# One Trainium2 core: the convolution's accumulator in two tiles, every second low half of the K and V weights by DMA, and the S5 bodies and the last V columns moved

## The chip, the cores and the metric

The kernel runs on one core of one Trainium2 chip. The metric is the time on the device in microseconds (us) of one execution; the kernel before was timed three times and the median is 2125.04 us (2120.92 to 2128.39). The engines of a core are TensorE (PE in the profile, PEld is its weight load), VectorE (DVE), ScalarE (ACT), GpSimd (POOL) and SyncE (SP), which here only starts transfers.

## The reference

One layer of a hybrid trunk in float32 over 256 tokens of width 2048: a gated convolution group and an S5 (state space) group side by side, attention to 256 memory tokens, and a layer of experts (PEER).

```python
hn = rms_norm(h, norm_mix_g)
proj = hn @ w_in                                  # 2048 -> 1024 conv_a, 1024 conv_gate, 1024 ssm_u
c = causal_depthwise_conv(conv_a * sigmoid(conv_gate), conv_w, conv_b)      # width 31, 1024 channels
c = layer_norm(c, conv_ln_g, conv_ln_b);  yc = c * sigmoid(c)
y = s5_scan(ssm_u) + d * ssm_u                    # complex states, 64 groups of 64
z = gelu(y);  ys = z * sigmoid(z @ ssm_glu_w)
h = h + concat([rms_norm(yc, g_conv), rms_norm(ys, g_ssm)]) @ w_out
mem_n = rms_norm(mem, mem_norm_g);  k, v = split(mem_n @ w_kv_mem)          # 2048 -> 2048 + 2048
h = h + softmax(q k / sqrt(512)) v @ w_o          # q from rms_norm(h) @ w_q_mem, 4 heads
h = h + peer(rms_norm(h))                         # 16 experts of 16384 for each of 8 heads and token
out = rms_norm(h, final_norm_g)
```

## The kernel before

Every large product goes through `linear()` (line 146). It takes a weight in columns of 512, and each column in tiles of two times 128 rows, 512 KB a tile. A tile is loaded by SyncE's queue into `w_raw` (five buffers, line 153). ScalarE rounds it to `w_hi` (line 162, three buffers), VectorE takes the difference `w_lo = w_raw - w_hi` (line 163, three buffers), and TensorE makes three products of each piece, high by high, low by high and high by low, into a PSUM tile `mm`: lines 172 to 174 where tokens are the rows of the result, lines 181 to 183 where channels are. Of the eight tiles of a column in w_in, K and V the last one is multiplied whole in float32 (lines 140 and 143), without a split.

Each engine runs its own instructions in a fixed order. That order is made when the program is built, by a scheduler that goes by priorities; the loads and splits of weights are lifted ahead of the matmuls by `AHEAD = 500`, the S5 work by `S5_AHEAD = 700`, and the convolution, which stands late in the code, fills what VectorE has free.

The front part of the kernel, up to the experts, runs through these stages: w_in (the S5 columns, then the convolution's columns and gate), the K columns from 191 us, the V columns, Gelu and the gate product of S5 (`ev_glu`, weight `ssm_glu_w`), the norm of the S5 group (`group_norm`, line 527), the first half of w_out's rows, which needs the S5 group alone (`korder` 4 to 7, result into `h1_dram`), the second half of w_out from 551 us, which needs the convolution's group, and then attention. The S5 group has eight bodies (`s5_body`, called by `s5_next()`), each of 128 channels: four were called among the w_in columns and one behind each of the four K columns. A body uses working tiles that go by tags, `s5a` to `s5d`, and its sine tables come from ScalarE.

The convolution (lines 560 to 576) is 31 steps for each of eight groups of 128 channels, 248 instructions on VectorE into one tile `acc` of eight groups. Then come a mean over the channels (`chan_sum`, matmuls with ones), the variance (`squares`, `chan_rstd`), Silu on ScalarE, and the group norm, whose rounded halves `aT_hi`, `aT_lo` are the upper part of the input of w_out (`yT`).

Of the kernel before, what the change touches and what calls it, by code (L numbers as in the profile page):

```python
# [9 lines left out]
F32 = mybir.dt.float32  # L10
# [10 lines left out]
P = 128  # L21
# [45 lines left out]
LAG = 2  # L67
R_BY = ('AAAA', 'AAVA')
# [3 lines left out]
def trunk(ctx, tc, a, out, dbg=None):  # L72
# [48 lines left out]
    with ExitStack() as wctx:  # L121
        atx = wctx.enter_context(ExitStack())
        wp = wctx.enter_context(tc.tile_pool(name="wp", bufs=3, side="right"))
# [22 lines left out]
        def linear(x, w, c0, ncol, evac, rows_out, kt=KT, korder=None, ahead=AHEAD, whole=None, cols=None):  # L146
            xh, xl = x
            js = korder or range(kt // KG)
            for n, (c, w_) in enumerate(cols or [(c, 512) for c in range(c0, c0 + ncol, 512)]):
                ncb = w_ // P  # L150
                ps = [psm.tile([P, 512] if rows_out else [P, 2, T], F32, name="mm", tag="mm") for _ in range(2)]
                for m, j in enumerate(js):
                    with tc.high_priority(offset=ahead):
                        raw = wp.tile([P, KG, w_], F32, name="w_raw", bufs=5)
                        SY.dma_start(raw, w[j * KG * P:(j + 1) * KG * P, c:c + w_].rearrange("(k p) c -> p k c", p=P))
# [40 lines left out]
        with ExitStack() as mctx:  # L196
# [316 lines left out]
            def squares(src):  # L513
                out = []
                for j in range(2):
                    t = s5w.tile([P, 4, T], F32, name="sqh", tag="s5b")
                    S.activation(t, src[:, 4 * j:4 * j + 4, :], AF.Square)
# [9 lines left out]
            def group_norm(src, col, hi, lo):  # L527
                r = chan_rstd(chan_sum(squares(src)))
                for j in range(2):
                    for q in range(4 * j, 4 * j + 4):  # L530
                        V.scalar_tensor_tensor(src[:, q, :], src[:, q, :], colv[:, col, q:q + 1], r, op0=ALU.mult,
                                               op1=ALU.mult)
                    split(hi[j], lo[j], src[:, 4 * j:4 * j + 4, :])
# [15 lines left out]
            group_norm(uT, 4, yT[0][2:], yT[1][2:])  # L549
# [10 lines left out]
            acc = mp.tile([P, CQ, T], F32, name="acc")  # L560
            for k in range(CW):
                for q in range(CQ):
                    src = cpad[:, q, k:k + T]
                    if k == 0:
                        V.tensor_scalar(acc[:, q, :], src, cwT[:, q, 0:1], colv[:, 0, q:q + 1], op0=ALU.mult,
                                        op1=ALU.add)
                    else:
                        V.scalar_tensor_tensor(acc[:, q, :], src, cwT[:, q, k:k + 1], acc[:, q, :],  # L568
                                               op0=ALU.mult, op1=ALU.add)
            mean = chan_sum([acc[:, :4, :], acc[:, 4:, :]])  # L570
            V.tensor_sub(acc, acc, bc(mean[:, None, :], [P, CQ, T]))
            r = chan_rstd(chan_sum(squares(acc)))
            V.tensor_mul(acc, acc, bc(r[:, None, :], [P, CQ, T]))
            for q in range(CQ):
                S.activation(acc[:, q, :], acc[:, q, :], AF.Silu, bias=colv[:, 2, q:q + 1],
                             scale=colv[:, 1, q:q + 1])
            group_norm(acc, 3, yT[0][:2], yT[1][:2])
# [575 lines left out]
```

## Time and profile before

| what | value |
|---|---|
| median of three runs | 2125.04 us (2120.92 to 2128.39) |
| the profiled execution | 2121.98 us |
| its span in the trace | 2120.0 us |
| granted clock of TensorE, mean | 0.972 |
| busy: TensorE, VectorE, ScalarE, GpSimd | 1970.8 (93%), 1760.7 (83%), 1024.5 (48%), 736.2 us (35%) |

The trace is of one execution; its times are from the span's start. The granted clock is the share of TensorE's full speed. Matmuls are pipelined, so the distance of two starts, not the length of one, is what a matmul takes. Shares over the whole span mix stages with different limits, so the stretches are read one by one.

### The profile page before, as it was taken

To read this page: it belongs to the slowest core of one execution; us is meant where nothing else is said; L and a number is where in the kernel's file an instruction comes from. 1 tells how busy PE (TensorE), PEld (TensorE's weight loads), DVE (VectorE), ACT (ScalarE), POOL (GpSimd) and SP (SyncE) were. 2 spreads that over 40 slices of the span, in tenths; PEclk is the share of its full clock that TensorE was granted. 3 is DMA by queue.
4 is the path that set the end of the run, shared out by engine and by line. 5 is a ranking of instruction groups with operands and counts; after the bars stand their busy time and mean duration, and the time that the engine had idled before them with its cause. 6 is when DMAs were issued, how large, how long until landed. Compare 5 with 4: busy or idle time off the path is not lost.

```text
span 2120.0 us, 32032 instructions
## 1 busy us (share of the span) xinstructions
PE 1970.8 (93%) x11619; PEld 1698.4 (80%) x11619; DVE 1760.7 (83%) x2855; ACT 1024.5 (48%) x1746; POOL 736.2 (35%) x548
## 2 busy tenths in 40 slices
PE   8998798999999999899999999689879999999997
PEld 7987786668799988788888888577667888888886
DVE  5789999987665566999986667998888999899997
ACT  5764544436454454333333333578793444444444
POOL 0000000000000002535446665543218877677772
PEclk9999989999999999999999999899999999999998
DMA  7554454554865476798999999998629999999995
GB/s 246 166 179 154 125 149 130 161 177 139 291 222 193 140 232 221 283 321 319 317 336 402 402 406 391 370 327 275 205 90 318 373 348 337 348 336 340 336 340 187
DMA packets 199390, 563.41 MB, mean 266 GB/s; under 512 B 32050, under 2 KB 40866, under 8 KB 199105
## 3 DMA queue, kind: packets, MB, share of 16 engines
q1 hardware_dynamic: 141888, 318.08, 45.5%
q0 software_dynamic: 57344, 243.30, 30.5%
q8 instruction: 91, 1.49, 0.3%
q14 instruction: 67, 0.54, 0.1%
HBM read 549.38 MB, written 11.93 MB: 265 GB/s over the span
## 4 chain that ended last, share of the span: by engine, by line
PE 48%; DVE 25%; issue 13%; POOL 6%; DMA 5%; ACT 2%; SPq 0%; DVEq 0%; POOLq 0%; ACTq 0%
PE acc L1100 8%; PE acc L1101 8%; PE acc L1099 8%; DVE u L861 6%; POOL u L859 5%; PE mm L183 4%; PE mm L181 4%; PE mm L182 4%; DVE acc L568 3%; DVE w_lo L163 3%; PE mm L174 2%; PE mm L173 2%; PE mm L172 2%; PE y L932 1%; DMA hnT<-ib_dram 1%
## 5 line engine op out<-in xcount | busy, mean ns | idle before, releaser
L861 DVE SCALAR_TENSOR_TENSOR u<-u,hnF 128x1280 f32<-128x1280 f32 x256 | 388.6, 1520 | 86.0 <-DMA u<-in_peer_u,uidx 84.6
L1064 POOL DMA_INDIRECT v<-in_peer_v,vidx x256 | 385.7, 1507 | 178.5 <-DVE accg L1066 68.5
L859 POOL DMA_INDIRECT u<-in_peer_u,uidx x256 | 308.1, 1204 | 328.2 <-DVE u L861 254.0
L162 ACT CAST w_hi<-w_raw 128x1024 fp32r<-128x1024 f32 (+2 forms) x228 | 231.4, 1018 | 289.1 <-PE mm L182 125.7
L901 PE MATMUL sy<-hnT,ut 128*128 128x256 f32 x1536 | 357.0, 385 | 7.9 <-ACT ut L897 7.3
L163 DVE TENSOR_TENSOR w_lo<-w_raw,w_hi 128x1024 fp32r<-128x1024 f32 (+2 forms) x228 | 270.8, 1190 | 111.5 <-ACT w_hi L162 111.3
L901 PEld LDWEIGHTS sy<-hnT,ut 128*128 128x128 f32 x1536 | 287.3, 193 | 48.6 <-ACT ut L897 11.9
L103 ACT CAST vh<-vr 128x1472 fp32r<-128x1472 f32 x128 | 183.2, 1431 | 271.0 <-PE acc L1100 165.8
L1100 PE MATMUL acc<-vh,wl 128*128 128x512 f32 (+1 forms) x768 | 296.7, 386 | 4.4 <-DVE wl L1090 4.3
L183 PE MATMUL mm<-aT_hi,w_lo 128*128 128x256 f32 x960 | 273.2, 293 | 27.2 <-DVE w_lo L163 27.1
L1101 PE MATMUL acc<-vl,wh 128*128 128x512 f32 (+1 forms) x768 | 295.9, 386 | 0.0
L742 POOL TENSOR_TENSOR hnT<-aT_hi,aT_lo 128x1024 f32<-128x1024 f32 (+1 forms) x2 | 3.8, 1908 | 814.5 <-ACT w_hi L162 814.5
L181 PE MATMUL mm<-aT_hi,w_hi 128*128 128x256 f32 x960 | 279.0, 294 | 4.0 <-DVE sg L264 2.3
L1099 PE MATMUL acc<-vh,wh 128*128 128x512 f32 (+1 forms) x768 | 276.5, 385 | 3.2 <-ACT vh L103 2.2
L182 PE MATMUL mm<-aT_lo,w_hi 128*128 128x256 f32 x960 | 276.4, 290 | 0.0
L104 DVE TENSOR_TENSOR vl<-vr,vh 128x1472 fp32r<-128x1472 f32 x128 | 216.5, 1692 | 39.6 <-ACT vh L103 36.9
L1066 DVE SCALAR_TENSOR_TENSOR accg<-v,coef,accg 128x576 f32<-128x576 f32 x256 | 208.7, 815 | 12.0 <-DMA v<-in_peer_v,vidx 7.4
L183 PEld LDWEIGHTS mm<-aT_hi,w_lo 128*128 128x128 f32 x960 | 185.5, 197 | 34.9 <-DVE w_lo L163 31.5
L181 PEld LDWEIGHTS mm<-aT_hi,w_hi 128*128 128x128 f32 x960 | 188.5, 197 | 8.3 <-DVE sg L264 2.9
L182 PEld LDWEIGHTS mm<-aT_lo,w_hi 128*128 128x128 f32 x960 | 189.0, 197 | 1.3 <-issue 0.4
L897 ACT COPY ut<-ut 128x768 f32<-128x768 f32 x128 | 100.4, 801 | 165.8 <-PE ut L895 145.9
L1100 PEld LDWEIGHTS acc<-vh,wl 128*128 128x128 f32 x768 | 145.2, 189 | 35.8 <-DVE wl L1090 5.4
(345 smaller groups left out, 3368.6 us busy)
## 6 DMA issues: line engine op xcount, KB each, us to landing
vr<-in_peer_v SPq DMA_DIRECT2D x128, 736.0 KB
raw<-in_peer_u SPq DMA_DIRECT2D x128, 384.0 KB
w_raw<-in_w_kv_mem SPq DMA_DIRECT2D x64, 512.0 KB
w_raw<-in_w_in SPq DMA_DIRECT2D x48, 512.0 KB
w_raw<-in_w_out SPq DMA_DIRECT2D x32, 512.0 KB
w_raw<-in_w_q_mem SPq DMA_DIRECT2D x32, 512.0 KB
w_raw<-in_w_o_mem SPq DMA_DIRECT2D x32, 512.0 KB
hnT<-ib_dram SPq DMA_DIRECT2D x18, 256.0 KB
```

The source lines that it names most:

```text
L162: S.copy(hi, raw)
L163: V.tensor_sub(lo, raw, hi.bitcast(F32))
L181: PE.matmul(o, wh, ah, start=first and cb % 2 == 0, stop=False, skip_group_check=True)
L182: PE.matmul(o, wh, al, start=False, stop=False, skip_group_check=True)
L183: PE.matmul(o, wl, ah, start=False, stop=last and end, skip_group_check=True)
L859: G.indirect_dma_start(out=u, out_offset=None, in_=a["peer_u"].rearrange("e (q c) -> (e q) c", c=GU), in_offset=bass.IndirectOffsetOnAxis( ...
L861: V.scalar_tensor_tensor(u, u, 1.0, hnF[:, self.tt, :], op0=ALU.mult, op1=ALU.mult, accum_out=self.act[:, j:j + 1])
L901: PE.matmul(ps[:, b % 2, :], ut[:, k, :], hnT[:, k, :], start=k == 0 and b % 2 == 0, stop=k == KD - 1 and b % 2 == 1, skip_group_check=True)
L1064: G.indirect_dma_start(out=v, out_offset=None, in_=table, in_offset=bass.IndirectOffsetOnAxis(ap=vidx[tt][:, j:j + 1], axis=0))
L1099: PE.matmul(o, wh[:, tt, :], vh[:, cs_], start=b == 0, stop=False)
L1100: PE.matmul(o, wl[:, tt, :], vh[:, cs_], start=False, stop=False)
L1101: PE.matmul(o, wh[:, tt, :], vl[:, cs_], start=False, stop=b == NB - 1)
```

## The change

`linear()` gets a parameter `dma_lo`, on for K and V alone. With it, every second tile of a column (`m` odd) that is split gets its low half in another way: ScalarE writes the negated rounded weight, as `lo = -raw` in the low half's type, and GpSimd starts a transfer that reads the same 512 KB of the weight again and adds it to `lo`. The number of buffers changes for all products: `w_raw` four instead of five, `w_lo` four instead of three. `s5_next()` is called once before the first w_in column of the convolution, so that each body comes one place earlier. Three V columns are made before the gate, and the fourth behind the S5 group's norm; V takes its tiles in the order 4 to 7, 0 to 3. The convolution's accumulator becomes two tiles of four groups: the lower in its old pool, the upper (`acc_late`) in the S5 tile of tag `s5c`. The steps that follow run for each half by itself.

```diff
+RAW_BUFS = 4
+HI_BUFS = 3
+LO_BUFS = 4
...
+                        raw = wp.tile([P, KG, w_], F32, name="w_raw", bufs=RAW_BUFS)
+                        src = w[j * KG * P:(j + 1) * KG * P, c:c + w_].rearrange("(k p) c -> p k c", p=P)
+                        SY.dma_start(raw, src)
...
-                        lo = wp.tile([P, KG, w_], F32R, name="w_lo")
+                        lo = wp.tile([P, KG, w_], F32R, name="w_lo", bufs=LO_BUFS)
                         S.copy(hi, raw)
-                        V.tensor_sub(lo, raw, hi.bitcast(F32))
+                        if dma_lo and m % 2:
+                            S.activation(lo, raw, AF.Copy, scale=-1.0)
+                            G.dma_start(lo, src, accum_op=ALU.add)
+                        else:
+                            V.tensor_sub(lo, raw, hi.bitcast(F32))
...
+            s5_next()
             for n in range(2):
                 run(linear(xT, a["w_in"], n * 512, 512, ev_a(n), False, whole=xW if W_IN else None))
                 s5_next()
...
-            for _ in linear(memT, a["w_kv_mem"], 0, D, ev_k, False, whole=memW if W_K else None):
+            for _ in linear(memT, a["w_kv_mem"], 0, D, ev_k, False, dma_lo=True, whole=memW if W_K else None):
                 s5_next()
-            kv_v = linear(memT, a["w_kv_mem"], D, D, ev_v, True, whole=memW if W_V else None)
-            run(kv_v)
+            kv_v = linear(memT, a["w_kv_mem"], D, D, ev_v, True, korder=[4, 5, 6, 7, 0, 1, 2, 3], dma_lo=True, whole=memW if W_V else None)
+            for _ in range(3):
+                next(kv_v)
...
+            group_norm([uT[:, :4], uT[:, 4:]], 4, yT[0][2:], yT[1][2:])
+            run(kv_v)
...
-            acc = mp.tile([P, CQ, T], F32, name="acc")
+            accs = [mp.tile([P, 4, T], F32, name="acc"), s5w.tile([P, 4, T], F32, name="acc_late", tag="s5c", bufs=1)]
             for k in range(CW):
                 for q in range(CQ):
-                    src = cpad[:, q, k:k + T]
+                    src, o = cpad[:, q, k:k + T], accs[q // 4][:, q % 4, :]
...
+            mean = chan_sum(accs)
+            for x in accs:
+                V.tensor_sub(x, x, bc(mean[:, None, :], [P, 4, T]))
+            r = chan_rstd(chan_sum(squares(accs)))
+            for j, x in enumerate(accs):
+                V.tensor_mul(x, x, bc(r[:, None, :], [P, 4, T]))
+                for q in range(4):
+                    S.activation(x[:, q, :], x[:, q, :], AF.Silu, bias=colv[:, 2, 4 * j + q:4 * j + q + 1],
+                                 scale=colv[:, 1, 4 * j + q:4 * j + q + 1])
+            group_norm(accs, 3, yT[0][:2], yT[1][:2])
```

The edits move instructions on every engine; three places show how. The first is VectorE's order at the end of the last S5 body (`zr`, `zi` are its states, the line that writes `uT` is its result, `zl` the low half of the gate's input). Before:

```order
L568 SCALAR_TENSOR_TENSOR acc<-cpad,cwT,acc 128x256 x3
L163 TENSOR_TENSOR w_lo<-w_raw,w_hi 128x1024
L461 TENSOR_TENSOR zr<-zr,sn 128x1024
L462 TENSOR_TENSOR zi<-zi,cs 128x1024
L163 TENSOR_TENSOR w_lo<-w_raw,w_hi 128x1024 x2
L469 SCALAR_TENSOR_TENSOR uT<-uT,colv,yp 128x256
L104 TENSOR_TENSOR zl<-uT,zh 128x1024
```

And now:

```order
L469 TENSOR_TENSOR zr<-zr,sn 128x1024
L470 TENSOR_TENSOR zi<-zi,cs 128x1024
L171 TENSOR_TENSOR w_lo<-w_raw,w_hi 128x1024
L577 TENSOR_SCALAR acc_late<-cpad,cwT,colv 128x256 x4
L579 SCALAR_TENSOR_TENSOR acc_late<-cpad,cwT,acc_late 128x256 x4
L477 SCALAR_TENSOR_TENSOR uT<-uT,colv,yp 128x256
L579 SCALAR_TENSOR_TENSOR acc_late<-cpad,cwT,acc_late 128x256 x9
```

Before, the convolution's steps (`acc`) stand ahead of the body's end and none follows it; now the steps of the upper half (`acc_late`) begin with the body's last two instructions and go on behind them.

The second is TensorE's order around the last channel sum of the convolution's norm (`chs_5099` before, `chs_5126` now). Before it stands among the tiles of the first half of w_out, ahead of the seventh of sixteen (`w_hi_4605`) and within it:

```order
L174 MATMUL mm_4566<-w_hi_4587,aT_lo2_4453 128x512
L510 MATMUL chs_5099<-sqh_5097,ones_68 128x256 x2
L172 MATMUL mm_4565<-w_hi_4605,aT_hi3_4450 128x512
L172 MATMUL mm_4566<-w_hi_4605,aT_hi3_4450 128x512
L510 MATMUL chs_5099<-sqh_5097,ones_68 128x256 x2
L173 MATMUL mm_4565<-w_lo_4606,aT_hi3_4450 128x512
```

Now `w_hi_4811` is the last of those sixteen tiles and `w_hi_5181` the first of the second half, whose input `aT_hi0` is the norm's result:

```order
L182 MATMUL mm_4753<-w_hi_4811,aT_lo3_4335 128x512
L180 MATMUL mm_4754<-w_hi_4811,aT_hi3_4331 128x512
L181 MATMUL mm_4754<-w_lo_4812,aT_hi3_4331 128x512
L182 MATMUL mm_4754<-w_hi_4811,aT_lo3_4335 128x512
L520 MATMUL chs_5100<-sqh_5098,ones_68 128x256 x2
L520 MATMUL chs_5126<-sqh_5122,ones_68 128x256 x4
L520 MATMUL chs_5126<-sqh_5124,ones_68 128x256 x4
L180 MATMUL mm_5177<-w_hi_5181,aT_hi0_4328 128x512
```

The last channel sum thus moved from the middle of the first half of w_out to its end, and with it the end of the sum before (`chs_5100`, the variance).

The third is ScalarE's order at the same place. Before, the squares (`sqh`), the square root (`ch_r_5108`) and the rounding of the norm's result (`aT_hi0`) stand among the roundings of w_out's first half:

```order
L517 ACTIVATE sqh_5097<-acc_4811 128x1024
L162 CAST w_hi_4605<-w_raw_4603 128x1024
L162 CAST w_hi_4623<-w_raw_4621 128x1024
L162 CAST w_hi_4651<-w_raw_4649 128x1024
L523 ACT_TABLE_LOAD
L523 ACTIVATE ch_r_5108<-chs_5099,eps_t_70 128x256
L162 CAST w_hi_4669<-w_raw_4667 128x1024
L103 CAST aT_hi0_4447<-acc_4811 128x1024
```

Now the roundings of three tiles of the second half stand ahead of the variance's square root (`ch_r_5109`) and of the eight Silu:

```order
L166 CAST w_hi_4811<-w_raw_4809 128x1024
L166 CAST w_hi_5181<-w_raw_5179 128x1024
L166 CAST w_hi_5199<-w_raw_5197 128x1024
L166 CAST w_hi_5217<-w_raw_5215 128x1024
L533 ACTIVATE ch_r_5109<-chs_5100,eps_t_70 128x256
L587 ACT_TABLE_LOAD
L587 ACTIVATE acc_4835<-acc_4835,colv_878 128x256 x4
L587 ACTIVATE acc_late_4836<-acc_late_4836,colv_878 128x256 x4
L527 ACTIVATE sqh_5122<-acc_4835 128x1024
```

So the Silu, which stood ahead of the squares and of the seventh tile's rounding before, now follow the rounding of the last tile and of three tiles beyond.

## Rows read from the trace of the kernel before

**Rows 1.** Busy time by stretch: start and end, length, busy us (instructions), granted clock, DMA share, GB/s.

```profile
20.00:140.00 120.00, 116.50 (x931) 109.22 (x930) 89.36 (x144) 72.71 (x121) 0.00 (x0) 0.99 0.64 190
160.00:180.00 20.00, 16.75 (x129) 14.13 (x127) 20.00 (x32) 5.34 (x9) 0.00 (x0) 0.91 0.45 152
191.00:468.00 277.00, 244.83 (x1526) 197.78 (x1525) 276.94 (x447) 124.08 (x163) 0.00 (x0) 0.94 0.50 151
468.00:551.00 83.00, 78.63 (x404) 66.49 (x401) 54.88 (x61) 46.70 (x54) 0.00 (x0) 0.98 0.51 170
551.00:605.00 54.00, 53.28 (x260) 43.27 (x259) 37.04 (x45) 28.89 (x43) 0.00 (x0) 1.00 0.92 304
605.00:860.00 255.00, 251.81 (x1716) 231.83 (x1716) 156.96 (x243) 121.33 (x177) 17.24 (x12) 0.99 0.60 199
```

**Rows 2.** TensorE's waits, 191 to 551 us: us in total, times, longest.

```profile
PE mm L183 <- DVE w_lo L163: 17.5, 8, 5.4
```

**Rows 3.** VectorE's timeline, S5 body beside convolution: start us, us, instruction.

```profile
270.91 1.21 DVE L163 TENSOR_TENSOR w_lo<-w_raw,w_hi 128x1024 fp32r<-128x1024 f32 x1
272.05 1.21 DVE L460 SCALAR_TENSOR_TENSOR t<-zi,sn 128x1024 f32<-128x1024 f32 x1
...
273.78 2.84 DVE L568 SCALAR_TENSOR_TENSOR acc<-cpad,cwT,acc 128x256 f32<-128x256 f32 x7
276.55 1.21 DVE L461 TENSOR_TENSOR zr<-zr,sn 128x1024 f32<-128x1024 f32 x1
```

**Rows 4.** ScalarE's groups, 191 to 468 us: busy us, mean ns | idle before.

```profile
L162 ACT CAST w_hi<-w_raw 128x1024 fp32r<-128x1024 f32 x60 | 62.7, 1046 | 98.4 <-PE mm L174 47.6 <-PE mm L182 45.6 <-DVE acc L565 1.8
...
L423 ACT ACTIVATE sn<-sn 128x1024 f32<-128x1024 f32 x5 | 5.3, 1060 | 0.1
```

**Rows 5.** TensorE's timeline within w_out's first half.

```profile
548.89 0.40 PE L173 MATMUL mm<-w_lo,aT_hi 128*128 128x512 f32 x1
549.12 0.40 PE L174 MATMUL mm<-w_hi,aT_lo 128*128 128x512 f32 x1
```

**Rows 6.** Line 859, 1000 to 1200 us: ns min/median/max, first and last start.

```profile
L859 POOL DMA_INDIRECT u<-in_peer_u,uidx x76: 932/939/2292, 1000.6 to 1197.2; - x76
```

**Rows 7.** The chain that ended last: two loads of 512 KB (start us, us).

```profile
163.47 4.52 DMA xc<-in_mem
...
574.85 9.16 DMA w_raw<-in_w_out
```

**Rows 8.** DMA queues, 191 to 468 us: packets, MB, share of 16 engines.

```profile
q1 hardware_dynamic: 21670, 41.48, 49.9%
```

**Rows 9.** ScalarE's timeline in the convolution's norm.

```profile
508.60 1.28 ACT L575 ACT_TABLE_LOAD   x1
509.89 4.05 ACT L575 ACTIVATE acc<-acc,colv 128x256 f32<-128x256 f32 x8
...
522.84 0.48 ACT L523 ACTIVATE ch_r<-chs,eps_t 128x256 f32<-128x256 f32 x1
```

**Rows 10.** VectorE's timeline in the convolution's norm.

```profile
505.14 2.28 DVE L573 TENSOR_TENSOR acc<-acc,ch_r 128x2048 f32<-128x2048 f32 x1
...
512.68 1.39 DVE L555 TENSOR_TENSOR xh<-xh,mm 128x512 f32<-128x512 f32 x2 [2.85 <-PE mm L174]
...
523.34 1.75 DVE L524 RECIPROCAL ch_r<-ch_r 128x256 f32<-128x256 f32 x1 [0.56 <-ACT ch_r L523]
525.13 3.26 DVE L531 SCALAR_TENSOR_TENSOR acc<-acc,colv,ch_r 128x256 f32<-128x256 f32 x8
```

**Rows 11.** TensorE's timeline at the S5 gate, and a channel sum.

```profile
470.92 0.50 PE L181 MATMUL mm<-zh,w_hi 128*128 128x256 f32 x2 [1.14 <-ACT zh L103]
...
473.27 0.42 PE L182 MATMUL mm<-zl,w_hi 128*128 128x256 f32 x1
473.48 0.42 PE L183 MATMUL mm<-zh,w_lo 128*128 128x256 f32 x1
...
520.27 1.03 PE L510 MATMUL chs<-sqh,ones 128*128 128x256 f32 x4
```

More of the change, by code (lines that the diff above doesn't have):

```diff
@@ L122, in trunk @@
         atx = wctx.enter_context(ExitStack())
-        wp = wctx.enter_context(tc.tile_pool(name="wp", bufs=3, side="right"))
+        wp = wctx.enter_context(tc.tile_pool(name="wp", bufs=HI_BUFS, side="right"))
         at = atx.enter_context(tc.tile_pool(name="at", bufs=1))
@@ L144, in whole_matmuls, with linear @@
                                   start=first and cb % 2 == 0, stop=last and cb % 2 == 1, skip_group_check=True)
-        def linear(x, w, c0, ncol, evac, rows_out, kt=KT, korder=None, ahead=AHEAD, whole=None, cols=None):
+        def linear(x, w, c0, ncol, evac, rows_out, kt=KT, korder=None, dma_lo=False, ahead=AHEAD, whole=None, cols=None):
             xh, xl = x
@@ L153, in linear @@
                     with tc.high_priority(offset=ahead):
-                        raw = wp.tile([P, KG, w_], F32, name="w_raw", bufs=5)
-                        SY.dma_start(raw, w[j * KG * P:(j + 1) * KG * P, c:c + w_].rearrange("(k p) c -> p k c", p=P))
+                        raw = wp.tile([P, KG, w_], F32, name="w_raw", bufs=RAW_BUFS)
+                        src = w[j * KG * P:(j + 1) * KG * P, c:c + w_].rearrange("(k p) c -> p k c", p=P)
+                        SY.dma_start(raw, src)
                         full = whole is not None and j >= kt // KG - NWHOLE
@@ L529, in group_norm @@
                 for j in range(2):
-                    for q in range(4 * j, 4 * j + 4):
-                        V.scalar_tensor_tensor(src[:, q, :], src[:, q, :], colv[:, col, q:q + 1], r, op0=ALU.mult,
+                    for q in range(4):
+                        o = src[j][:, q, :]
+                        V.scalar_tensor_tensor(o, o, colv[:, col, 4 * j + q:4 * j + q + 1], r, op0=ALU.mult,
                                                op1=ALU.mult)
-                    split(hi[j], lo[j], src[:, 4 * j:4 * j + 4, :])
+                    split(hi[j], lo[j], src[j])
             zs = ([s5w.tile([P, 4, T], F32R, name="zh", tag="sn") for _ in range(2)],
@@ L558, in trunk @@
             run(linear(yT, a["w_out"], 0, D, ev_half, True, korder=list(range(4, 8))))
-            acc = mp.tile([P, CQ, T], F32, name="acc")
+            accs = [mp.tile([P, 4, T], F32, name="acc"), s5w.tile([P, 4, T], F32, name="acc_late", tag="s5c", bufs=1)]
             for k in range(CW):
                 for q in range(CQ):
-                    src = cpad[:, q, k:k + T]
+                    src, o = cpad[:, q, k:k + T], accs[q // 4][:, q % 4, :]
                     if k == 0:
-                        V.tensor_scalar(acc[:, q, :], src, cwT[:, q, 0:1], colv[:, 0, q:q + 1], op0=ALU.mult,
-                                        op1=ALU.add)
-                    else:
[L568 to L577, printed above, removed]
+                        V.tensor_scalar(o, src, cwT[:, q, 0:1], colv[:, 0, q:q + 1], op0=ALU.mult, op1=ALU.add)
+                    else:
+                        V.scalar_tensor_tensor(o, src, cwT[:, q, k:k + 1], o, op0=ALU.mult, op1=ALU.add)
+            mean = chan_sum(accs)
[4 more added lines that the diff above has]
+                V.tensor_mul(x, x, bc(r[:, None, :], [P, 4, T]))
+                for q in range(4):
+                    S.activation(x[:, q, :], x[:, q, :], AF.Silu, bias=colv[:, 2, 4 * j + q:4 * j + q + 1],
+                                 scale=colv[:, 1, 4 * j + q:4 * j + q + 1])
+            group_norm(accs, 3, yT[0][:2], yT[1][:2])
         at2 = wctx.enter_context(tc.tile_pool(name="at2", bufs=1, side="right", reuse_waits="tile"))
```

3 lines of the change are left out of this document (1 added, 2 removed).

## Prediction

> **What bounds the kernel now.** I read the busy time by stretch first, then who waits for whom in the stretch that is not full of matmuls, then the groups of instructions there, and last the timeline at the places the change moves. In the busy time by stretch [rows 1] the reader is to see one stretch that behaves unlike the others. From 551 to 860 us TensorE is busy 53.28 of 54 and 251.81 of 255 us. From 191 us, where the K projection begins, to 551 us, where the second half of w_out begins, it is busy 244.83 + 78.63 = 323.46 of 360 us. That leaves 36.5 us idle, and the granted clock, 0.94 and then 0.98, is 0.95 on the mean, so some 18 us more went at the lower of the two levels. VectorE explains it: it is busy 276.94 of the 277 us from 191 to 468, and then only 54.88 of the 83 us to 551. TensorE's waits name it too: the longest entry is 17.5 us in eight waits on w_lo [rows 2]. So VectorE sets the pace up to 468 us and has a third of its time free behind that, while TensorE has work in both. The gain to be had here is the 36.5 us and part of the 18; 860 us onward (the PEER part) starts when this front part ends, and shifts with it.
>
> TensorE's true work in 191 to 551 is thus 323.5 - 18 = 305.5 us, and VectorE's is 276.94 + 54.88 = 331.8 us.
>
> **The change, part by part.** *Low halves by DMA.* K and V have four columns of 512 each, seven split tiles a column, of which three (every second place) lose their VectorE subtraction: 24 in all. One costs 1.14 us, from one start to the next (w_lo at 270.91, the next at 272.05) [rows 3]. VectorE loses 24 x 1.14 = 27.4 us, and 331.8 becomes 304.4 us. ScalarE gains 24 negations of the shape of the cast, 1046 ns each [rows 4], 25 us; it is busy 124.08 + 46.70 of 360 us [rows 1], so this is hidden unless it stands in front of a cast that TensorE needs (below). 24 transfers of 512 KB are added on GpSimd's queue, which is empty here [rows 1].
>
> No row shows an accumulating transfer. Its time is bounded by when it may start and when it is needed. It has four w_lo buffers: the negation waits until TensorE is through with the fourth split tile before, and behind it three tiles of 12 matmuls of 0.235 us run (548.89 to 549.12) [rows 5], 8.5 us in all. Of these go a cast (1.05, it stands ahead in ScalarE's order), the negation (1.05), and the issue on GpSimd (0.94 us for a gather) [rows 6]. 5.4 us are left for the landing. A plain 512 KB load took 4.52 us where DMA was 0.45 busy and one took 9.16 us in the stretch where it is 0.92 busy [rows 1, 7]. Below the first I do not go, since an add must move at least as many bytes. DMA load in the stretch is 49.9% for 41.48 MB in 277 us [rows 8], so 1.75 us of all 16 engines per 512 KB; 24 transfers add 42 us at one pass and 84 us at two, which takes the share from 0.5 to between 0.65 and 0.8. I take a landing of 6.4 us, nearer the half-busy row than the loaded one, so 1.0 us too late. About half of the 24 have an S5 body's matmuls or the whole fp32 tile among the three tiles and are covered; the other 12 cost 12 us. The ends are 0 and 48 us (3.8 us for 12, 0.26 for the rest).
>
> The Trainium skill ("Collectives: The Full Stack", the section on the bandwidth ceiling) says that an add in the DMA engines is slower than a copy not for the add but because it needs two source reads. No row here shows an add. By it my estimate would be one more pass of 1.75 us on the 4.52 us load, 6.3 us, and the sum would stay as it is; it speaks against the lower end, where the transfer costs as much as a copy.
>
> *Upper half of the convolution in an S5 tile.* 124 of the 248 steps can only run when the last S5 body has freed its tile. At 0.396 us each (273.78 to 276.55 for seven) [rows 3] that is 49 us of VectorE work taken out of the full stretch and put behind it, where 28 us of VectorE were free and the last V column now also stands. *S5 one place ahead* and *V's last column behind the gate* fit to this: VectorE's order shows the two first S5 bodies where they were and the eighth earlier, and TensorE keeps a column of work (22 us) to do beside the S5 gate and its norm, which cost it nothing before either. The sums of the two engines are then 304.4 us (VectorE) against 305.5 us (TensorE), spread alike. TensorE becomes the bound, with VectorE so close behind that stalls stay. In 20 to 140 us, where VectorE is busy 74%, TensorE loses 3.5 us idle and some 1.2 us of clock in 120 [rows 1], 4%. I take the same here: 12 us. Its ends are 9 us (3%, below the row, if the extra buffer of w_lo helps) and the 54 us lost now.
>
> *What is late next: the convolution's norm.* Before, the last channel sum of this norm ran while ten tiles of the first half of w_out were still to come, so its steps between 505 and 531 us [rows 10] were covered. In the changed order the convolution ends late: the mean stands four tiles before the end of that half, the variance sum ends behind its last tile, and nothing else is left for TensorE until the first upper-part tile can use the result. From that last tile on: two xh additions 1.39 and a w_lo 1.14 that VectorE does first, reciprocal 1.75, first half of the product 1.14 (half of 2.28), eight Silu 4.05, two squares of 1.06 as the other activations of that size [rows 4], a table load 1.28 (beside the last channel sums), square root 0.48, reciprocal 1.75, eight scalings 3.26, the low half 1.21 as a w_lo [rows 3, 9, 10]. That is 19.6 us; with some 1 us of hand-overs 20.5 us in which TensorE stands still. After TensorE had waited at 471 us (1.14 us in the row shown) and had gone on, its 128x256 matmuls went from 473.27 us at 0.21 us, where half of the 0.235 us above is 0.12 [rows 11]; fifteen of them at that rate cost 1.4 us, and for a longer wait I add 2 us here.
>
> *Buffers.* Four w_raw instead of five and four w_lo instead of three hold for all later projections too. Four tiles ahead are 11.3 us against the 9.16 us of the slowest load [rows 7], so I cost it at nothing; the bounds are -4 us (TensorE's idle time from 551 to 860) and +6 us (two tiles late).
>
> *Sum.* 305.5, less 2.1 us of channel sum that now lies in the gap (eight matmuls, four of them 1.03 us [rows 11]), is 303.4; + 20.5 + 2 + 12 + 12 = 349.9 us instead of 360. The gain is 10.1 us. The profiled execution took 2121.98 us (span 2120.0 us), which gives 2112; it was 3 us below the median of the three runs, 2125.04, and from there it gives 2115. I say 2113.
>
> **Rivals.** *The adding transfer lands too late (slower).* Place: every second K and V tile; TensorE needs the low half at the third matmul of a tile, and all that follows in its order waits. At the 9.16 us of the loaded row the sum is 303.4 + 22.5 + 12 + 48 = 386 us, 26 more than now: 2149. It decides from the landing on at which 12 tiles lose 22 us, 5.4 + 1.8 = 7.2 us. For it: DMA share rises well over the half. Against it: a 512 KB load at half load took 4.52 us.
>
> *All is hidden (faster by more).* Landing within 5.4 us and 3% of stalls: 303.4 + 22.5 + 9 = 335 us, 25 less: 2098. For it: TensorE's idle time has one releaser, w_lo, and that falls by 27 us. Against it: two engines with the same sum in fixed orders.
>
> *No change.* Each S5 body puts four full-size ScalarE activations of 1.06 us [rows 4] and mostly a table load of 1.28 us [rows 9] in a row before a cast. With VectorE as the bound this did not show. TensorE as the bound has two tiles, 5.6 us, less a cast, and loses some 1.2 us in each of eight: 10 us more, 360 us, 2122 to 2125.
>
> **How the numbers follow.** I give my forecast 0.40 (2104 to 2119 by itself), all hidden 0.20, no change 0.18, late transfer 0.22. Less than 0.3%, 6.4 us, can't be told from no change. The forecast counts as faster except for its upper end (0.04), the no-change case as same but for 0.02. Faster 0.56, same 0.20, slower 0.24. The range for eight in ten goes from 2094, a little beyond "all hidden", to 2142, into the late transfer, whose last part is left out with the end where even the gap closes (2088).
>
> **What would show it.** VectorE below 100% between 191 and 470 us, and TensorE there with few waits on w_lo from VectorE: the sum of the two engines was right. Waits of TensorE that a w_lo transfer ends, about 1 us and about a dozen: the landing; several us for each K and V tile: the late transfer. One wait of about 20 us of TensorE before the second half of w_out, with ScalarE's Silu and the reciprocals in it: the gap. The PEER part from its first gather to the end as long as before. I am wrong if the gap isn't there, or if TensorE's losses in K and V stay as large as now.

## The result and the profile after

The changed kernel took 2098.41 us (median of four, 2097.61 to 2105.12) beside 2126.06 us for the kernel before (2120.92 to 2128.39, four runs); the ratio is 0.9866, 95% interval 0.9843 to 0.9888. It is 27.7 us faster; the forecast was 12 from the median shown. The time lies in the range given, the direction is right, and the gain is more than twice the one forecast.

The profiled execution was the longest of the four, 2105.12 us, with a span of 2103.4 us. So the time of one mark inside the trace, the first gather of the experts' part, is used beside the medians below. Before, then after, from each trace's view of tile `u` (ns min/median/max, first and last start):

```profile
L859 POOL DMA_INDIRECT u<-in_peer_u,uidx x256: 932/939/2296, 839.0 to 1520.7; - x128
```

```profile
L871 POOL DMA_INDIRECT u<-in_peer_u,uidx x256: 935/940/2276, 817.0 to 1505.8; - x128
```

Up to there the changed kernel is 22.0 us ahead. Behind it the profiled executions took 1281.0 us (2120.0 - 839.0) before and 1286.4 us after. The busy time by stretch, from the K projection to the second half of w_out, with the columns of [rows 1]:

```profile
190.00:400.00 210.00, 201.99 (x1364) 164.34 (x1364) 195.66 (x301) 129.76 (x169) 25.57 (x21) 0.98 0.81 215
400.00:464.00 64.00, 61.95 (x355) 52.62 (x354) 60.61 (x114) 35.35 (x39) 3.62 (x3) 1.00 0.71 197
464.00:509.00 45.00, 45.00 (x195) 36.34 (x193) 37.51 (x58) 17.45 (x17) 0.00 (x0) 1.00 0.76 253
509.00:530.00 21.00, 6.39 (x18) 4.82 (x18) 10.22 (x14) 10.71 (x16) 0.00 (x0) 0.75 0.71 215
```

The reader is to see that VectorE, full from 191 to 468 us before, is now idle for 14.3 of 210 us, and that TensorE loses little up to 509 us and nearly everything in the 21 us behind it. TensorE's waits from 188 to 532 us (us in total, times, longest) answer to [rows 2]:

```profile
PE chs L520 <- ACT sqh L527: 9.5, 1, 9.5
PE mm L181 <- DMA w_lo<-in_w_kv_mem: 6.1, 3, 2.9
PE mm L180 <- ACT aT_hi L106: 5.1, 1, 5.1
PE mm L191 <- DVE w_lo L171: 2.5, 1, 2.5
PE mm L191 <- DMA w_lo<-in_w_kv_mem: 1.2, 2, 0.8
```

Before, VectorE's low halves had a second entry from 191 to 551 us, on the lines where tokens are the rows of the result:

```profile
PE mm L173 <- DVE w_lo L163: 10.5, 4, 5.5
```

So the 28.0 us of waits on VectorE's low halves (17.5 + 10.5, in twelve) became 2.5 in one; five waits on transfers, 7.3 us, are new; two long ones, 9.5 and 5.1 us, belong to the norm of the convolution. TensorE's timeline shows the latter, the hole before w_out's second half, with ScalarE and VectorE around its channel sum:

```profile
518.43 1.04 ACT L527 ACTIVATE sqh<-acc_late 128x1024 f32<-128x1024 f32 x1
518.57 5.88 PE L520 MATMUL chs<-sqh,ones 128*128 128x256 f32 x16 [9.47 <-ACT sqh L527]
524.49 0.47 ACT L533 ACTIVATE ch_r<-chs,eps_t 128x256 f32<-128x256 f32 x1 [3.72 <-PE chs L520]
526.78 1.67 DVE L542 SCALAR_TENSOR_TENSOR acc<-acc,colv,ch_r 128x256 f32<-128x256 f32 x4
529.59 0.64 PE L180 MATMUL mm<-w_hi,aT_hi 128*128 128x512 f32 x1 [5.14 <-ACT aT_hi L106]
```

From 509.1 us (518.57 - 9.47) to 529.59 are 20.5 us, of which 5.9 are channel sums, at the lower of the two clock levels in part (granted clock 0.75 in this stretch). Where the stretch begins is set in each trace by the same matmuls, the last whole tile of w_in: 193.69 us before and 192.94 after, so that 191 becomes 190.25 (start us, us):

```profile
192.94 1.89 PE L146 MATMUL mm<-x_whole,w_raw 128*128 128x256 f32 x8
```

From there to w_out's second half it took 339.3 us (529.6 - 190.25) instead of 360; the forecast was 349.9. To see what is left beside work and hole, the work needs a correction. The forecast took the channel sum that moved into the hole as eight matmuls of the trace, 2.1 us. The program's eight matmuls are sixteen records there, as before, where two sums follow each other:

```profile
490.41 3.62 PE L510 MATMUL chs<-acc,ones 128*128 128x256 f32 x16
493.87 1.89 PE L510 MATMUL chs<-sqh,ones 128*128 128x256 f32 x8
```

From start to start the sum takes 3.5 us (493.87 - 490.41). So the work is 302.0 us (305.5 - 3.5, an estimate like the 305.5) instead of 303.4, and 16.8 us are left (339.3 - 302.0 - 20.5).

### The profile page after: what moved, and what is told of

It is laid out like the page before. It is cut to its first block, busy times and chain, and to the rows that moved or that the text cites. A ratio compares the mean times of both kernels' runs of the same rounds, so it can differ in the third digit from the quotient of the medians.

```text
span 2103.4 us, 32088 instructions
## 1 busy us (share of the span) xinstructions
PE 1961.3 (93%) x11619; PEld 1690.5 (80%) x11619; DVE 1730.8 (82%) x2833; ACT 1047.1 (50%) x1770; POOL 765.6 (36%) x572
## 4 chain that ended last, share of the span: by engine, by line
PE 48%; DVE 20%; issue 14%; DMA 8%; POOL 6%; ACT 3%; SPq 0%; POOLq 0%; DVEq 0%; ACTq 0%
PE acc L1112 8%; PE acc L1113 8%; PE acc L1111 8%; DVE u L873 6%; POOL u L871 6%; PE mm L181 4%; PE mm L180 4%; PE mm L182 4%; PE mm L191 3%; PE mm L189 3%; PE mm L190 3%; DMA w_lo<-in_w_kv_mem 2%; DVE w_lo L171 2%; DMA hnT<-ib_dram 1%; DVE acc L579 1%
## 5 line engine op out<-in xcount | busy, mean ns | idle before, releaser
L171 DVE TENSOR_TENSOR w_lo<-w_raw,w_hi 128x1024 fp32r<-128x1024 f32 (+2 forms) x204 | 240.2, 1179 | 105.8 <-ACT w_hi L166 105.5
L189 PEld LDWEIGHTS mm<-aT_hi,w_hi 128*128 128x128 f32 x960 | 184.2, 192 | 8.6 <-ACT w_hi L166 4.7
L190 PEld LDWEIGHTS mm<-aT_lo,w_hi 128*128 128x128 f32 x960 | 184.6, 192 | 2.4 <-issue 1.2
L169 POOL DMA_DIRECT2D w_lo<-in_w_kv_mem x24 | 29.2, 1216 | 417.0 <-ACT w_lo L168 342.8
```

What stands on the lines that cost most here:

```text
L189: PE.matmul(o, wh, ah, start=first and cb % 2 == 0, stop=False, skip_group_check=True)
L190: PE.matmul(o, wh, al, start=False, stop=False, skip_group_check=True)
```

## Experiments

Each kernel was timed beside the kernel before. "First gather" is from its profiled execution, and "behind" is its span less that.

| run | median us (runs) | ratio to before, 95% | first gather | behind |
|---|---|---|---|---|
| changed | 2098.41 (4) | 0.9843 to 0.9888 | 817.0 | 1286.4 |
| e1 no transfers into w_lo | 2115.81 (5) | 0.9949 to 0.9976 | 825.5 | 1287.2 |
| e2 transfers alone | 2112.95 (5) | 0.9939 to 0.9966 | 821.8 | 1286.8 |
| e3 both accumulators early | 2121.13 (11) | 0.9970 to 0.9990 | 836.5 | 1283.6 |
| e4 more transfers | 2099.24 (4) | 0.9878 to 0.9909 | 817.4 | 1279.0 |
| e5 V columns in front | 2109.33 (6) | 0.9918 to 0.9953 | 820.3 | 1282.0 |
| e6 no S5 body ahead | 2095.62 (4) | 0.9842 to 0.9877 | 815.8 | 1280.1 |
| e7 three w_lo buffers | 2123.78 (12) | 0.9983 to 1.0003 | 840.0 | 1285.3 |
| e8 GpSimd subtracts | 2095.58 (5) | 0.9854 to 0.9888 | 812.6 | 1278.9 |
| e9 five w_lo buffers | 2095.58 (4) | 0.9850 to 0.9883 | 814.9 | 1278.4 |
| e10 five, more transfers | 2102.20 (6) | 0.9871 to 0.9919 | 822.8 | 1281.6 |
| e11 buffers alone | 2128.03 (12) | 1.0007 to 1.0027 | 838.3 | 1281.1 |
| e12 copy, not add | 2089.40 (4) | 0.9824 to 0.9852 | 804.9 | 1282.2 |
| e13 copy, three buffers | 2093.51 (4) | 0.9836 to 0.9876 | 809.1 | 1280.7 |
| e14 copy, both early | 2116.99 (10) | 0.9950 to 0.9975 | 830.6 | 1284.4 |
| e15 norm lifted | 2093.83 (5) | 0.9839 to 0.9879 | 807.6 | 1282.0 |
| e16 five and three groups | 2105.80 (6) | 0.9897 to 0.9928 | 816.0 | 1285.0 |
| e17 changed, again | 2092.73 (5) | 0.9843 to 0.9885 | 810.4 | 1278.8 |
| e18 before, again | 2127.95 (1) | | 842.7 | 1283.3 |

### How far one execution speaks

*e17 and e18: the two kernels again, with no edit.*

> The changed kernel, nothing altered. Theory A (the front part is the same in every execution and the experts' part scatters by 1278 to 1287 us, the ends seen in the profiles so far): first gather at 815 to 819 us whatever the time; median 2096 to 2102. Theory B (the front part itself scatters with the landings): the first gather moves by more than 4 us from 817.0.

> The kernel before, nothing altered. Theory A: first gather at 837 to 841 us, and the experts' part between 1278 and 1288 us. Theory B: the first gather moves by more than 4 us from 839.0.

The first gather came at 810.4 us instead of 817.0, so the front part itself scatters (theory B for the changed kernel); before it moved by 3.7 us. TensorE's waits of the second execution:

```profile
PE chs L520 <- ACT sqh L527: 9.5, 1, 9.5
PE mm L180 <- ACT aT_hi L106: 5.1, 1, 5.1
PE mm L191 <- DVE w_lo L171: 2.5, 1, 2.5
PE mm L191 <- DMA w_lo<-in_w_kv_mem: 1.6, 3, 0.7
PE mm L181 <- DMA w_lo<-in_w_kv_mem: 1.4, 1, 1.4
PE mm L189 <- DVE sg L272: 0.3, 1, 0.3
```

Hole and stalls are the same; the waits on transfers are 3.0 us instead of 7.3. The whole tile of w_in stands at 195.04 us there and the hole ends at 523.18, so the stretch took 330.8 us (523.18 - 192.35), of which 20.0 are the hole and 8.8 are left beside work and hole. Of the 8.5 us between the two executions 4.3 are waits on transfers, and 3.8 are a longer busy time of TensorE up to the hole (308.8 and 305.0 us, at a granted clock of 0.98 and 0.99); that the lower clock comes from the waits is likely, but not shown. So the landings are what moves most in the front part of the changed kernel. By two executions each, it is ahead by 27 us at the first gather (840.9 - 813.7), as in the medians, and the experts' part is the same in the mean (1282.2 and 1282.6). The pooled median of nine runs of the changed kernel is 2098.1. Differences below some 5 us are not told apart here.

### Which part pays

*e1*, K and V without the parameter; *e2*, the parameter and the buffers in the kernel before; *e11*, the buffers alone in the kernel before:

```diff
-            for _ in linear(memT, a["w_kv_mem"], 0, D, ev_k, False, dma_lo=True, whole=memW if W_K else None):
+            for _ in linear(memT, a["w_kv_mem"], 0, D, ev_k, False, whole=memW if W_K else None):
...
```

> The changed kernel with every low half of K and V taken by VectorE again; all else as changed. Theory A (the relief of VectorE is what pays): VectorE has 24 x 1.14 = 27.4 us more between 190 and 530 us; it was idle there for 36 us, of which 10.8 in the gap before w_out's second half, so a part is absorbed: I expect 10 to 20 us more than the changed kernel, 2108 to 2118, with TensorE waiting for w_lo from VectorE by 10 us or more again and no wait on a transfer into w_lo. Theory B (the places of the V column, the S5 bodies and the upper accumulator pay, the transfers only trade VectorE's time for late landings): within 4 us of the changed kernel, 2095 to 2102.

> The kernel before with the low halves of every second K and V tile by transfer (and four buffers of w_raw and w_lo, as in the change), nothing moved, one accumulator. Theory A: the stretch from 191 to 468 us, where VectorE is busy all the time, shrinks by most of 27.4 us, down to TensorE's own work; the convolution's norm stays covered, so there is no gap of 20 us before w_out's second half: 18 to 27 us less than before, 2099 to 2108. Theory B: at most a third of the gain, 2117 or more, since the transfers' landings (7 us of waits in the changed kernel) take the rest.

> The kernel before with four buffers of w_raw and four of w_lo, and nothing else of the change. Theory A (a buffer matters only where a transfer's landing has to be led): VectorE stays busy all the time up to 468 us, no change, 2121 to 2128. Theory B (the fourth w_lo buffer itself lets VectorE work further ahead, and a part of the 17.5 us of waits goes): 2112 to 2119, so that it would make up the gain seen without the transfers.

Without the transfers 17.4 us are lost, with nothing but them 11.3 are gained, and the moves alone (e1) bring 8.4: together the two halves give more than their sum, 19.7. e1's time fell where theory A had it, with 7.2 us of waits on VectorE's low halves where A had 10 or more; e2 fell between the two. Its VectorE is no longer full from 191 to 468 us, but TensorE keeps 7.4 us of waits on VectorE and 10.8 on transfers:

```profile
PE mm L188 <- DVE w_lo L168: 7.4, 5, 3.2
PE mm L178 <- DMA w_lo<-in_w_kv_mem: 6.2, 4, 2.5
PE mm L188 <- DMA w_lo<-in_w_kv_mem: 4.6, 2, 3.2
```

The buffers alone gain nothing (e11, even 4 us slower than the kernel before beside it). The four `w_raw` buffers and V's order of tiles were not tried by themselves.

*e5*, `run(kv_v)` ahead of the gate; *e6*, without the first `s5_next()`:

> The changed kernel with all four V columns ahead of the S5 gate again. Before, 11.7 us lay between the gate's last matmul and w_out's first (489.2 to 500.9 us), most of it filled with channel sums of the convolution. Theory A (the column only moves a hole): TensorE stands still some 10 us at the S5 group's norm, in which VectorE goes on with the convolution, so that the hole of 20.5 us before w_out's second half shrinks by about as much: 2096 to 2104. Theory B (the column is cover that the changed kernel gains from): the hole at the S5 norm comes on top, 8 to 12 us more than the changed kernel, 2106 to 2110.

> The changed kernel without the additional S5 body ahead of the convolution's columns. Theory A: the scheduler puts the bodies by their priority, and TensorE's order among the K and V tiles stays the same, so nothing changes: 2094 to 2102. Theory B (the body one place ahead lets the last one end earlier, and with it the gate and the upper half of the convolution): one body's time on VectorE (some 14 us) later, 5 to 14 us more, 2103 to 2112.

e5 bears out theory B in its median, 11 us more than the changed kernel; the mark in its trace says 3.3, which is within the scatter. The hole is now at the S5 norm, and that at the convolution is gone:

```profile
463.12 3.78 PE L519 MATMUL chs<-sqh,ones 128*128 128x256 f32 x8 [5.14 <-ACT sqh L526]
474.58 0.79 PE L180 MATMUL mm<-w_hi,aT_hi 128*128 128x512 f32 x1 [7.67 <-ACT aT_hi L106]
```

The S5 body ahead is worth nothing (e6, theory A).

### What a landing costs

*e12*, a plain copy in place of the add; *e7*, `LO_BUFS = 3`; *e9*, `LO_BUFS = 5`:

```diff
-                            G.dma_start(lo, src, accum_op=ALU.add)
+                            G.dma_start(lo, src.bitcast(F32R))
```

> The changed kernel with each transfer into w_lo a plain copy of the weight in place of an add, so that the low half holds other numbers; all instructions, places and waits stay. It measures what the adding costs. Theory A (an add is slower in the DMA engines than a copy of 512 KB): a copy lands in 4.5 to 6 us from its issue in place of 7 to 9.5, TensorE's waits on it fall from 7.3 us to below 2: 2091 to 2095, and the DMA share between 190 and 400 us falls from 0.81 toward 0.65. Theory B (adding costs no more than copying): same waits, 2096 to 2101, same DMA share.

> The changed kernel with three w_lo buffers instead of four, so that each transfer into w_lo can be started one tile (2.8 us) later than now. In the changed kernel a transfer takes 7 to 9.5 us from its issue and five of 24 keep TensorE waiting, 7.3 us together. Theory A (a landing of this length is hidden by the tile of lead that the fourth buffer gives): most of the 24 are now late, by up to 2.8 us each: 10 to 40 us more, 2108 to 2138. Theory B (the lead is set by something else, such as the wait for the other buffers or ScalarE): no change, 2095 to 2102.

> The changed kernel with five w_lo buffers. With three, fifteen of the 24 transfers kept TensorE waiting, 32.1 us together; with four it is five and 7.3 us. Theory A (the buffer sets the lead of a transfer): one more tile of lead, at most one or two late ones are left, 4 to 7 us less than the changed kernel, 2091 to 2095. Theory B (with four the rest of the waits come from the load of w_raw and ScalarE's place in the order): no change, 2096 to 2101.

With the copy no wait on a transfer is left among TensorE's waits, and the median is 8.7 us below the pooled 2098.1, somewhat under theory A's range:

```profile
PE chs L520 <- ACT sqh L527: 9.5, 1, 9.5
PE mm L180 <- ACT aT_hi L106: 5.1, 1, 5.1
PE mm L191 <- DVE w_lo L171: 2.5, 1, 2.5
PE mm L189 <- DVE sg L272: 1.1, 1, 1.1
```

The stretch is 327.5 us (517.75 - 190.25), 11.8 less than in the first execution of the changed kernel and 3.3 less than in the second. Work and hole (19.95) taken off, 5.5 us are left. Its four runs lie within 1.2 us of each other, the nine of the changed kernel within 13.7: with the add's landings the scatter is gone too. The DMA queues from 190 to 400 us (packets, MB, share of 16 engines), add and copy:

```profile
q1 hardware_dynamic: 17777, 34.05, 49.2%
q0 software_dynamic: 5650, 10.91, 31.1%
```

```profile
q1 hardware_dynamic: 18633, 35.68, 51.1%
q0 software_dynamic: 5712, 11.01, 19.3%
```

GpSimd's queue `q0` carries the transfers into w_lo. Per 512 KB (0.524 MB) the add occupied the 16 engines for 3.1 us (0.311 x 210 x 0.524 / 10.91), the copy for 1.9, and a load on `q1` for 1.6. The Trainium skill ("Collectives: The Full Stack", the section on the bandwidth ceiling) says that an add needs two source reads. The trace agrees in the size: my estimate by it was one more pass of 1.75 us, and 1.2 to 1.5 were measured. The median from issue to landing is 4.8 us for the copy and 7.8 for the add in e9 (the profile gives none for the changed kernel). In the changed kernel's chain of waits five transfers took 6.9 to 9.5 us from their issue on; two of them:

```profile
290.45 6.93 DMA w_lo<-in_w_kv_mem
333.29 9.46 DMA w_lo<-in_w_kv_mem
```

The fourth buffer is what gives them their lead: with three, fifteen of the 24 are late and the whole gain is gone, as theory A said:

```profile
PE mm L191 <- DMA w_lo<-in_w_kv_mem: 18.4, 8, 4.3
PE mm L181 <- DMA w_lo<-in_w_kv_mem: 13.7, 7, 3.4
PE mm L181 <- DVE w_lo L171: 1.1, 1, 1.1
```

A fifth buffer leaves 8.0 us of such waits in six, so it does not take the rest away; its median, between the two theories, is within the scatter.

### Why TensorE hardly waits for VectorE

*e13*, the copy with three buffers; *e3* and, with the copy, *e14*: the upper accumulator in the early pool.

```diff
-            accs = [mp.tile([P, 4, T], F32, name="acc"), s5w.tile([P, 4, T], F32, name="acc_late", tag="s5c", bufs=1)]
+            accs = [mp.tile([P, 4, T], F32, name="acc"), mp.tile([P, 4, T], F32, name="acc_late")]
```

> The copy in place of the add (the low half holds other numbers) with three w_lo buffers instead of four. With the copy and four buffers TensorE waited 2.5 us for w_lo of VectorE and not at all on a transfer: 2089. Theory A (slack of VectorE keeps the stalls small): waits on w_lo from VectorE stay below 5 us; what comes is at most a few landings, 2089 to 2097. Theory B (the fourth buffer keeps them small): VectorE's part comes back to some 12 us, 2099 to 2105.

> The copy in place of the add with the upper accumulator in the lower one's pool, so that its steps fill VectorE from the start; four w_lo buffers. Theory A (slack): VectorE is busy over 98% from 190 to 400 us, and TensorE waits again, on w_lo and on the S5 bodies: 10 us or more between 190 and 464 us, with the low clock in the stretch where it stands; against that the hole of 20 us is gone: 2095 to 2112. Theory B (the buffer): no stalls and no hole, 2068 to 2075.

> The changed kernel with the upper accumulator in the pool of the lower one, so that its steps need not wait for the last S5 body. The convolution can start its upper half early and fills VectorE; in TensorE's order its last channel sum stands ahead of the thirteenth of sixteen tiles of w_out's first half. Theory A (the gap of 20.5 us is a real cost of the late upper half): the gap closes in part, and VectorE is full again up to the S5 gate; the two engines have sums of 304 and 306 us, so the stretch takes 315 to 335 instead of 340 us: 2078 to 2093. Theory B (the late upper half is what keeps VectorE from holding up K and V): TensorE's waits on w_lo come back and the time is 2098 to 2115.

Without the fourth buffer the waits on VectorE's low halves stay at 0.6 us (e13, theory A). But ten waits on transfers, 9.2 us, came in, and they give VectorE time as well (the wait on the squares in the hole fell from 9.5 to 2.7 us), so e13 speaks against the buffer as the reason without settling it. With the convolution free to run early they return (e14), and the time is even above theory A's range. The stretches 190 to 400 and 400 to 464 us of e14, and its waits from 190 to 464:

```profile
190.00:400.00 210.00, 198.00 (x1318) 165.32 (x1316) 210.00 (x365) 131.82 (x173) 14.99 (x21) 0.99 0.71 224
400.00:464.00 64.00, 44.12 (x292) 34.85 (x293) 46.94 (x68) 19.03 (x20) 0.70 (x1) 0.71 0.29 90
```

```profile
PE mm L191 <- DVE w_lo L171: 12.9, 8, 5.8
PE yp L474 <- DVE t L467: 8.3, 2, 7.2
```

VectorE is full up to 436 us, the last S5 bodies (`yp`) and the low halves behind them are late, and TensorE is idle 20 of 64 us at a granted clock of 0.71. e3 is much the same with the add, and missed both theories: the hole at the convolution is gone, and between 400 and 464 us TensorE is idle for 20 us (busy 43.97, granted clock 0.76). What the late accumulator does is thus to keep the convolution's steps away from VectorE while the S5 bodies and the low halves need it. Whether it does so by the order of the instructions or by the time it leaves VectorE free was not taken apart.

### What the hole is worth

*e4*, `dma_lo=True` for the S5 gate and w_out's first half; *e10*, this with five buffers and no S5 body ahead; *e8*, GpSimd subtracts there; *e15*, the norm at a higher priority (with `LO_BUFS = 5`, no S5 body ahead); *e16*, one upper group accumulated early (what follows `#` names the run and is not in the kernel):

```diff
+                        elif g_lo and m % 2:                                  # e8
+                            G.tensor_sub(lo, raw, hi.bitcast(F32))
...
+            with tc.high_priority(offset=700):                                # e15
+                mean = chan_sum(accs)
...
+            mid = mp.tile([P, 1, T], F32, name="acc_mid")                     # e16
+            late = s5w.tile([P, 3, T], F32, name="acc_late", tag="s5c", bufs=1)
```

> The changed kernel with every second low half of the S5 gate's weight and of w_out's first half by transfer too: 4 + 8 tiles, 12 x 1.14 = 13.7 us less for VectorE between 400 and 510 us, where the upper half of the convolution runs. Theory A: the convolution ends some 10 us earlier and the gap of 20.5 us before w_out's second half shrinks by as much, less 2 to 4 us of late landings: 2089 to 2094. Theory B (the DMA engines, 0.76 busy there, can't take 12 transfers more): TensorE waits for w_lo or w_raw, 2098 to 2106.

> Five w_lo buffers, the low halves of the S5 gate and w_out's first half by transfer as in the run before with 36 transfers, and no additional S5 body in front. There the hole before w_out's second half had shrunk by 9 to 10 us, but 21.4 us of waits on transfers had come in. Theory A (lead): these waits fall to below 8 us and the shrunk hole is what remains: 2080 to 2089. Theory B (the DMA engines are 0.94 busy behind 464 us, and the landings grow with it): the waits stay above 15 us, 2093 to 2100.

> The changed kernel, in which every second low half of the S5 gate's weight and of w_out's first half (12 tiles) is a subtraction on GpSimd, which has no other work there, instead of on VectorE. No bytes are added. Theory A (the hole of 20.5 us before w_out's second half is VectorE's work on the upper half of the convolution, ended too late): 13.7 us less for VectorE between 400 and 510 us, the hole shrinks by 8 to 13 us: 2085 to 2092. Theory B (GpSimd's subtraction, 1.9 us for an addition of this size in the trace of before, is late itself or holds VectorE up): 2096 or more.

> The changed kernel with five w_lo buffers, without the additional S5 body, and with the convolution's norm (mean to group norm) at a priority 700 higher. In the changed kernel the squares were done at 498.9 us, but the variance's last sums stood behind the last tile in TensorE's order and ran at 508. In the new order they stand ahead of it. Theory A (the hole is made by that place): the variance is ready some 3 us earlier, and the hole shrinks by 2 to 5 us: 2088 to 2093. Theory B (the hole is made by the convolution's end on VectorE): 2093 to 2098, as with five buffers alone.

> The changed kernel without the additional S5 body and with one of the four upper groups of the convolution accumulated early (five groups in the early pool, three in the S5 tile): 31 steps of 0.396 us, 12.3 us of VectorE's work, go from behind the last S5 body to ahead of it, into its 14 us of slack. Theory A (slack and hole can be traded): the hole shrinks by 8 to 12 us, the S5 bodies slip by a few: 2086 to 2094. Theory B (the slack is what keeps the S5 bodies on time): the last body comes after the gate's first tiles, TensorE waits there for about what the hole gives back, 2094 to 2102.

e4 took theory B's time: the 9.5 us wait in the hole is gone, and 21.4 us of waits on transfers are there instead, 14.1 of them on the twelve new ones:

```profile
PE mm L181 <- DMA w_lo<-in_w_out: 7.9, 4, 2.9
PE mm L191 <- DMA w_lo<-in_ssm_glu_w: 6.2, 2, 3.5
PE mm L191 <- DMA w_lo<-in_w_kv_mem: 5.2, 4, 1.8
```

A fifth buffer did not help (e10, theory B and a little above it). e8 ended between its theories: the wait in the hole fell to 1.3 us, but VectorE lost what it had been relieved of. Its timeline and GpSimd's at the same time:

```profile
406.74 1.21 DVE L173 TENSOR_TENSOR w_lo<-w_raw,w_hi 128x1024 fp32r<-128x1024 f32 x1
407.87 8.31 DVE L581 SCALAR_TENSOR_TENSOR acc_late<-cpad,cwT,acc_late 128x256 f32<-128x256 f32 x10
```

```profile
406.59 3.62 POOL L171 TENSOR_TENSOR w_lo<-w_raw,w_hi 128x1024 fp32r<-128x1024 f32 x1 [3.17 <-ACT w_hi L166]
412.06 2.65 POOL L171 TENSOR_TENSOR w_lo<-w_raw,w_hi 128x1024 fp32r<-128x1024 f32 x1 [1.85 <-ACT w_hi L166]
```

Ten steps of the convolution took 8.31 us beside GpSimd's two subtractions, where ten took 4.05 in the changed kernel. e15's order shortens the wait in the hole from 9.5 to 5.6 us, as theory A said, but its time lies in theory B's range: its first gather, 807.6 us, is the earliest with the add, and its median, 2093.83, is no further from e17's than the scatter. e16 gave theory B's time or more: the last S5 body slipped, TensorE waited for more transfers (10.2 us), and its last wait in the hole was still 6.2 us. Apart from the copies, whose low halves hold other numbers, no version here is shown to be faster than the changed kernel.

## Why the prediction was right or wrong

- *What bounds, and VectorE's relief.* Right. VectorE left 100%, and TensorE's waits on its low halves went from 28.0 to 2.5 us. Without the 24 transfers 17.4 us are lost (e1).
- *The hole at the convolution's norm.* Right in place. That its size is right too, 20.5 us forecast and 20.5 and 20.0 measured in the two executions, is in part luck: errors cancel. The forecast had only a table load, 1.28 us, between the squares and the square root, with the channel sum beside it; from the squares' end (519.47) to the square root (524.49) it was 5.0 us, since the sixteen matmuls of the sum went on until then (518.57 to 524.45). Against that, four of the eight scalings stand ahead of the first rounding, 1.7 us instead of 3.3, and 1.1 us of VectorE's first work was done before the hole began. The clock's 2 us came, but behind this stretch: from 529.59 us eight matmuls went at 0.43 us, some 1.6 us more than at 0.235.
- *Late landings.* 12 us forecast. Against the copy, the changed kernel's stretch has 11.3 us more beside work and hole in its first execution (16.8 - 5.5) and 3.3 in the second (8.8 - 5.5); the medians say 8.7. So the term is the upper end of what occurs. One landing was sized about right: 7.3 us from the issue on by the forecast (0.94 + 6.4), 7.8 in the median of e9. How many are late was off: not twelve by 1 us, but four or five by 0.3 to 2.9.
- *Stalls: the step that failed.* I took "4%, the same here: 12 us" from 20 to 140 us. With the copy, where no landing is late, 5.5 us are left beside work and hole, 3.6 of them two waits on VectorE. So the term was more than twice too large. The row that it was taken from could not give it. Of the 3.5 us of idle time there, only 0.9 were waits on VectorE's low halves; 1.0 each were a wait on the convolution's weights and one on ScalarE's rounding. From TensorE's waits before, 20 to 140 us:

```profile
PE mm L183 <- DVE w_lo L163: 0.9, 2, 0.5
```

VectorE's busy share alone does not set the stalls: the row had 74%, and with the copy VectorE is 97% busy from 190 to 400 us (204.24 of 210) and 98% to 464 (62.45 of 64). What keeps them small is the late accumulator, which takes 124 convolution steps away from there: where these run early, 12.9 us of such waits come back (e14). By which of its effects it does so, order or free time, stays open.

- *S5 one place ahead*, costed at nothing: right (e6). *The last V column* covers the S5 norm, as said; in front it costs 11 us by the median (e5).
- *Buffers at nothing.* Alone they gain nothing (e11). But the fourth w_lo buffer, which I took for the lead of the transfers without a price, is worth some 25 us with them (e7).
- *The sum.* In the mean of the two executions the stretch took 335.1 us, 14.8 less than the 349.9 forecast. Of these, 6.5 are the stalls (12 - 5.5), 4.7 the landings (12 against 7.3 in the mean), 2 the clock that falls behind the stretch, 1.4 the channel sum taken too short, and the rest the hole. The stretch thus gives 24.9 (360 - 335.1) of the 27 us at the first gather; the 2 that remain are within the scatter. The experts' part is as long as before in the mean, as forecast.
- *The rivals.* "All is hidden" named the time, 2098, by other terms: it had stalls of 9 us and no landing cost, and there are 5.5 and 3 to 11. "Late transfer" is what three buffers bring (2123.78). "No change", by ScalarE's runs ahead of casts, does not show: no wait on `w_hi` is left among TensorE's waits.

## What to carry to other kernels

When the full engine is relieved and its remaining work moved off the critical stretch, don't carry a stall share over from another stretch by its busy share: look up who was waited for in that stretch, and ask what work still competes with what the bound engine needs. A transfer that must land before a tile is used needs a buffer more of lead; and where the DMA engines got 0.97 busy by them (464 to 510 us in e4), further transfers cost what they saved. A mark inside the trace, in two executions, tells the front's gain from the scatter of the rest.

## What the runs showed of the hardware

- A subtraction of two SBUF tiles on GpSimd (3.19 us on the mean) and VectorE's convolution steps, which also read two tiles, hardly ran side by side: ten steps took 8.31 us instead of 4.05, and for 5.0 of the 8.31 us GpSimd's two subtractions ran. The Trainium skill ("SBUF — State Buffer", the section "Who interferes with whom") says that a VectorE instruction with two SBUF inputs contends with a GpSimd instruction that reads SBUF; the trace agrees. It is not always VectorE that loses: its own subtraction at 406.74 us kept its 1.21 us beside GpSimd's, which took 3.62.
- An accumulating transfer of 512 KB took GpSimd 1203 ns to issue, a copy 703 ns, and 3.1 against 1.9 us of all 16 DMA engines.
